# A two-layer encoder trunk: x and memory channels-first from the host, token sums by squares and a ones product, parameters packed as columns

## The chip, the core and the metric

The kernel runs on one core of a Trainium2 chip. The metric is the time of one execution on the device in microseconds, the median of the runs shown; lower is better.

## What is computed

A trunk of two layers over 256 tokens of 2048 channels (fp32), with 256 memory tokens of 2048 channels. Each layer normalises x, forms one wide projection, feeds four branches (RWKV-7 in both directions, differential attention, latent attention, attention into memory), gates them, projects each, merges them with sigmoid gates, projects again and adds the result to x. The reference, cut:

```python
def _rms_norm(t, g):
    return t * lax.rsqrt(jnp.mean(t * t, axis=-1, keepdims=True) + NORM_EPS) * g

for l in range(DEPTH):                       # DEPTH = 2
    h = _rms_norm(x, norm_g[l])
    p = h @ w_in[l]                          # 2048 -> 14784 columns, split into the branches' inputs and gates
    y_a = _rwkv7_bidir(rw_u, ...)
    y_b = ...                                # differential attention
    y_c = _mla(...)
    mem_n = _rms_norm(mem, mem_norm_g[l])    # the same memory tokens in both layers, another gain
    y_d = _mem_attention(m_q, mem_n, mem_w_kv[l], mem_qk_g[l])
    z = sum(sigmoid(merges[b]) * ((y_b_ * silu(gates[b])) @ w_branch[l, b]) for b in range(4))
    x = x + z @ w_out[l]
```

## The kernel before

**The stream of products.** `main` walks a list of jobs (`jobs`): the memory keys (memk, 16 blocks of 128 channels, 512 columns), the memory values (memv), then the products of the normalised x (U, which feeds RWKV, first), and so on through both layers. For two blocks at a time raw weights come by one 512 KB DMA on SyncE's queue (`raww`, 3 buffers, line 543). ScalarE rounds each block to `whi` (128x512) and VectorE takes the rest into `wlo`; five of each are in flight (`LOOK`). The activations are split in the same way (S0 to S3 and S4 to S7 for the memory, T1h and T1l for x), and three matmuls of hi and lo stand for one fp32 product. So a block costs six matmuls of 512 columns, or twelve of 256 in the jobs where weights are the stationary side (`product`, line 156 for every matmul; transposes are on line 161).

**What runs beside it.** Seven generators (norms, prep, xs, tables, attention, latent, rw) are stepped by a meter of the time issued so far; `yield` hands over, and a tile scheduler then orders each engine's queue by a simulated timeline. Each engine runs its own queue strictly in order. All VectorE and ScalarE work carries line 95, the meter's, so it is told apart by tile names.

**Memory.** `mem_prep` loads the memory token-major in four DMAs of 512 KB on ScalarE's queue (three into U, one into ygh), transposes 128x128 pieces on TensorE into a PSUM bank pa, and splits each into S with the gain `gains` as scale (64 transposes in two layers, of the same memory). The memory norm's scale `mrs` is not applied to S; squares of the token-major rows are summed by ScalarE (scratch T1l), and `mrs` multiplies the finished products raw and V.

**x in layer 0.** `x_prep` waits until block 3 of the memory is split, loads x token-major into Z on ScalarE's queue (line 417), sums squares on ScalarE (scratch T1h), multiplies the rows by their scale, transposes 32 pieces on TensorE and splits each from PSUM into T1h and T1l, 256 columns at a time. Layer 1 takes the same path from the x that layer 0 left on the chip. The transposes stand between the matmuls of memv and of the first U job.

**Parameters.** `params` gathers 14 small arrays as rows by GpSimd DMAs, transposes them once, and copies them to `cols`; gains are turned in the same way. The identity and other constants (`cst`) come in two DMAs at the start.

## Time and profile before

| | before |
|---|---|
| runs | 2080.51, 2083.33, 2084.84 us; median 2083.33 us |
| profiled execution: span on the core | 2081.6 us, 34016 instructions |
| its own time outside the span | not kept apart; the span lies between the lowest and the highest run |
| TensorE busy | 2052.8 us (99%), 12158 matmuls and transposes |
| VectorE, ScalarE, GpSimd busy | 68%, 54%, 6% |
| chain that ended last | TensorE 86%, issue 6%, DMA 4%, VectorE 2%, ScalarE 1% |
| DMA | 364.20 MB, mean 175 GB/s |

Busy time is the time in which an engine executes; the chain that ended last follows the work back from the last instruction, at each step to what released it. An engine that is 99% busy leaves 28.8 us of the span in which it waits; these lie in a few places, and each is read where it stands.

### The profile page before, as it was taken

The numbers are of one execution on the slowest core, as the hardware profiler recorded it, in microseconds if no ns is written. First come the engines' busy times: TensorE is split into PE (matmuls) and PEld (weight loads), VectorE is DVE, ScalarE is ACT, GpSimd is POOL, SyncE is SP. The second block draws the span as 40 slices with busy tenths as digits, with TensorE's granted clock in tenths as the row PEclk, the third lists the DMA queues.
The fourth block names the chain that finished last, engine by engine and source line by source line (L and its number), as shares of the span: only waits on it lengthen the run. The fifth ranks groups of instructions, "written<-read, shape, count | busy, mean of one in ns | idle before, by whom it ended". The sixth has DMA issues, their size and how long they took to land.

```text
span 2081.6 us, 34016 instructions
## 1 busy us (share of the span) xinstructions
PE 2052.8 (99%) x12158; PEld 1699.6 (82%) x12158; DVE 1419.1 (68%) x3073; ACT 1127.8 (54%) x2333; POOL 133.6 (6%) x168
## 2 busy tenths in 40 slices
PE   8999999999999999999999999999999999999999
PEld 6998897777877877778889988877778778777887
DVE  6787888886677577465665657666656866665654
ACT  6756575555555454445565566665555545444543
POOL 3000010110000010000000000010011001000000
PEclk9999999999999999999999999999999999999999
DMA  7655655556466566556766556555565655664565
GB/s 251 184 173 157 184 168 162 156 171 178 139 183 170 154 184 194 153 170 219 223 191 179 175 160 174 156 157 167 154 177 148 190 146 156 191 185 142 174 218 185
DMA packets 220313, 364.20 MB, mean 175 GB/s; under 512 B 40854, under 2 KB 59344, under 8 KB 219824
## 3 DMA queue, kind: packets, MB, share of 16 engines
q1 hardware_dynamic: 216528, 355.25, 58.5%
q10 hardware_dynamic: 2560, 6.30, 0.8%
q8 instruction: 95, 1.56, 0.3%
q0 software_dynamic: 1056, 0.49, 0.2%
q14 instruction: 74, 0.61, 0.1%
HBM read 354.64 MB, written 11.53 MB: 176 GB/s over the span
## 4 chain that ended last, share of the span: by engine, by line
PE 86%; issue 6%; DMA 4%; DVE 2%; ACT 1%; SPq 0%; POOL 0%; POOLq 0%; DVEq 0%; ACTq 0%
PE mm L156 75%; PE pr L156 5%; PE pa L156 3%; PE pa L161 2%; DMA BK<-sp 1%; DMA sp<-sc 1%; DVE wlo L95 1%; DMA raww<-in_mem_w_kv 1%; DMA sc<-S 0%; PE pr L161 0%; ACT whi L95 0%; DMA raww<-in_w_in 0%; DVE Z L95 0%; DVE sg L95 0%; DMA U<-in_mem 0%
## 5 line engine op out<-in xcount | busy, mean ns | idle before, releaser
L95 DVE TENSOR_TENSOR wlo<-raww,whi 128x512 fp32r<-128x512 f32 (+2 forms) x1300 | 863.7, 673 | 483.6 <-ACT whi L95 475.2
L95 ACT ACTIVATE whi<-raww 128x512 fp32r<-128x512 f32 (+2 forms) x1300 | 788.2, 617 | 730.1 <-PE mm L156 478.0
L156 PE MATMUL mm<-whi,T1l 128*128 128x512 f32 (+2 forms) x1472 | 574.8, 394 | 0.0
L156 PE MATMUL mm<-wlo,T1h 128*128 128x512 f32 (+2 forms) x1440 | 570.2, 396 | 0.5 <-DVE wlo L95 0.4
L156 PE MATMUL mm<-whi,T1h 128*128 128x512 f32 (+2 forms) x1472 | 533.6, 391 | 2.7 <-ACT whi L95 2.7
L156 PEld LDWEIGHTS mm<-whi,T1h 128*128 128x128 f32 x1472 | 278.0, 190 | 65.2 <-ACT whi L95 5.7
L156 PEld LDWEIGHTS mm<-wlo,T1h 128*128 128x128 f32 x1440 | 271.1, 188 | 62.6 <-DVE wlo L95 5.8
L156 PEld LDWEIGHTS mm<-whi,T1l 128*128 128x128 f32 x1472 | 276.5, 188 | 53.7 <-issue 2.0
L156 PE MATMUL mm<-T1l,whi 128*128 128x256 f32 x960 | 271.9, 284 | 0.0
L156 PE MATMUL mm<-T1h,wlo 128*128 128x256 f32 x960 | 270.0, 283 | 1.0 <-DVE wlo L95 0.9
L156 PE MATMUL mm<-T1h,whi 128*128 128x256 f32 x960 | 270.1, 283 | 0.0
L156 PEld LDWEIGHTS mm<-T1h,wlo 128*128 128x128 f32 x960 | 180.5, 189 | 2.3 <-DVE wlo L95 1.1
L156 PEld LDWEIGHTS mm<-T1h,whi 128*128 128x128 f32 x960 | 180.3, 188 | 1.5 <-issue 0.3
L156 PEld LDWEIGHTS mm<-T1l,whi 128*128 128x128 f32 x960 | 180.3, 188 | 1.3 <-issue 0.3
L156 PE MATMUL mm<-whi,ygh 128*128 128x512 f32 (+1 forms) x296 | 114.2, 404 | 6.1 <-ACT ygh L95 4.0
L156 PE MATMUL mm<-wlo,ygh 128*128 128x512 f32 (+1 forms) x296 | 118.5, 401 | 0.1
L156 PE MATMUL mm<-whi,ygl 128*128 128x512 f32 (+1 forms) x296 | 116.9, 397 | 0.0
L179 POOL TENSOR_TENSOR small<-small,cst 128x4 f32<-128x4 f32 (+3 forms) x46 | 52.1, 1134 | 563.5 <-DVE small L95 543.8
L156 PE MATMUL mm<-whi,S 128*128 128x512 f32 x256 | 85.0, 408 | 1.2 <-ACT S L95 0.9
L156 PEld LDWEIGHTS mm<-whi,ygh 128*128 128x128 f32 x296 | 56.6, 192 | 20.7 <-ACT ygh L95 4.6
L156 PEld LDWEIGHTS mm<-wlo,ygh 128*128 128x128 f32 x296 | 56.8, 192 | 12.4 <-DVE wlo L95 0.5
L156 PEld LDWEIGHTS mm<-whi,ygl 128*128 128x128 f32 x296 | 56.8, 192 | 12.1
(281 smaller groups left out, 2182.5 us busy)
## 6 DMA issues: line engine op xcount, KB each, us to landing
raww<-in_w_in SPq DMA_DIRECT2D x432, 512.0 KB, 3.7
raww<-in_w_branch SPq DMA_DIRECT2D x64, 512.0 KB, 3.8
raww<-in_w_out SPq DMA_DIRECT2D x64, 512.0 KB, 3.9
raww<-in_mem_w_kv SPq DMA_DIRECT2D x32, 512.0 KB, 3.8
raww<-in_w_in SPq DMA_DIRECT2D x16, 384.0 KB, 3.2
raww<-in_w_in SPq DMA_DIRECT2D x16, 320.0 KB, 3.1
raww<-in_w_in SPq DMA_DIRECT2D x16, 256.0 KB, 3.2
Z<-in_x ACTq DMA_DIRECT2D x2, 1024.0 KB, 7.8
```

Source lines behind the costliest of these rows:

```text
L95: return g(out, *args, **kw)
L156: self.nc.tensor.matmul(out, lhsT=lhsT, rhs=rhs, start=start, stop=stop)
L161: self.nc.tensor.transpose(out, in_, self.ident[:k, :k])
L179: self.nc.gpsimd.tensor_tensor(ss, ss, self.cst[:, C_MH:C_MH + n], op=ALU.pow)
```

## The change

The host hands in xT and memT, [128, 16, 256] each: channel on the partition, block of channels, token. It also hands in all of a layer's parameters as one array of columns (pcols) and both gains as columns (gcols).

- `params`: one DMA of `cols` instead of 14, a transpose and a copy. `mem_prep`: one DMA of `gains` instead of two, two transposes and two copies per layer. `setup`: `cst` comes in one DMA, issued behind the first memory loads; `ones` is now 128x2; an Exp on it stands at the start.
- `mem_prep`: X0 to X3 hold the memory channels-first and are split into S straight from SBUF; no transposes, in both layers.
- `channel_sums` (new): per quarter of the channels a square on ScalarE (128x1024), a sum over four blocks on VectorE that reads with a stride of 256 elements, a sum of the four quarters, and a product with `ones` on TensorE that sums over the partitions. It runs for x (scratch T1h, behind the load of xT) and, when that has ended (`xsum`), for the memory (scratch T1l).
- `x_first` (new, layer 0 only): four DMAs of xT into Z; sums; the scale is spread over the tokens by a copy and two transposes and copied to `r4` (named r in rows); 16 VectorE operations multiply each block by gain and scale; then eight splits of 512 columns, T1h on ScalarE, T1l on VectorE. `("hT", 0)` opens the U job when all of this has been issued.

Layer 1's `x_prep`, the jobs and their order in `jobs` are unchanged. The diff, cut to its core:

```diff
     def setup(self):
-        with self.tc.high_priority(2 * HP):
-            nc.sync.dma_start(self.cst[:, :128], a["consts"][:, :128])
-        nc.sync.dma_start(self.cst[:, 128:], a["consts"][:, 128:])
...
-        self.ones = self.cp.tile([128, 1], F32, name="ones")
+        self.ones = self.cp.tile([128, 2], F32, name="ones")
         nc.gpsimd.memset(self.ones, 1.0)
+        with self.tc.high_priority(2 * HP):
+            nc.scalar.activation(self.small(2), self.ones, AF.Exp)
...
     def params(self, l):
-        rows = self.t("kkn", [128, 256])[:P_N, :128]
-        def put(off, ap):
-            q.dma_start(rows[off:off + ap.shape[0]], ap)
-        put(P_SH, a["rw_shift"][l].rearrange("j (i p) -> (j i) p", p=128))
...
-        yield PD if l == 0 else 25.0
-        ps = self.pa()[:, :P_N]
-        self.tr(ps, rows)
         cols = self.t("cols", [128, P_N + 29])
-        nc.vector.tensor_copy(cols[:, :P_N], ps)
+        q.dma_start(cols[:, :P_N], a["pcols"][l])
+        yield PD if l == 0 else 25.0
...
     def mem_prep(self, l):
-        X3 = self.t("U", [128, 3, 2, 512])
-        X = [X3[:, j] for j in range(3)] + [self.t("ygh", [128, 2, 512])]
+        X3 = self.t("U", [128, 3, 4, 256])
+        X = [X3[:, j] for j in range(3)] + [self.t("ygh", [128, 4, 256])]
...
-            nc.sync.dma_start(rows[0], a["mem_norm_g"][l].rearrange("(k p) -> k p", p=128))
+            nc.sync.dma_start(g, a["gcols"][l])
...
-        mem = a["mem"][0].rearrange("(t p) n -> p t n", p=128)
-        q.dma_start(X[0], mem[:, :, 0:512])
+        mem = a["memT"]
+        for h in range(2):
+            q.dma_start(X[0][:, 2 * h:2 * h + 2], mem[:, 2 * h:2 * h + 2])
...
         for j in range(4):
-            for k2 in range(2):
-                i = 2 * j + k2
-                if i in (0, 2, 4):
-                    q.dma_start(X[i // 2 + 1], mem[:, :, i * 256 + 512:i * 256 + 1024])
-                ps = self.pa().rearrange("p (k t) -> p k t", k=2)
-                for k in range(2):
-                    kk = j * 4 + k2 * 2 + k
-                    for tt in range(2):
-                        self.tr(ps[:, k, tt * 128:tt * 128 + 128],
-                                X[j][:, tt, (k2 * 2 + k) * 128:(k2 * 2 + k) * 128 + 128])
-                    with self.tc.high_priority(2 * HP if kk < 4 else 0):
-                        self.split(T[j][:, k2 * 2 + k], T[4 + j][:, k2 * 2 + k], ps[:, k], scale=g[:, kk:kk + 1])
+            if j < 3:
+                q.dma_start(X[j + 1], mem[:, 4 * j + 4:4 * j + 8])
+            if j == 0 and l == 0:
+                nc.sync.dma_start(self.cst, a["consts"])
+            for k in range(4):
+                kk = j * 4 + k
+                with self.tc.high_priority(2 * HP if kk < 4 else 0):
+                    self.split(T[j][:, k], T[4 + j][:, k], X[j][:, k], scale=g[:, kk:kk + 1])
+                self.ev.add(("mT", l, kk))
...
-        yield from self.until("xsumsq")
-        ss = self.t("mss", [128, 2, 2])
-        jk = self.t("T1l", [128, 4096])
...
+        yield from self.until("xsum")
+        ss = self.t("mss", [128, 2])
+        yield from self.channel_sums(X, self.t("T1l", [128, 4096]), ss)
+        self.v["mrs"] = ss
...
+    def channel_sums(self, X, jk, rs):
+        nc = self.nc
+        sq = jk[:, 0:2048].rearrange("p (a n) -> p a n", a=2)
+        part = jk[:, 2048:3072].rearrange("p (j t) -> p j t", j=4)
+        acc = jk[:, 3072:3328]
+        for j in range(4):
+            with self.tc.issue_after(self.last[0]):
+                nc.scalar.activation(sq[:, j % 2], X[j].rearrange("p k t -> p (k t)"), AF.Square)
+            yield
+            with self.tc.issue_after(self.last[1]):
+                nc.vector.tensor_reduce(part[:, j], sq[:, j % 2].rearrange("p (k t) -> p t k", k=4), axis=AX.X,
+                                        op=ALU.add)
+            yield
+        nc.vector.tensor_reduce(acc, part.rearrange("p j t -> p t j"), axis=AX.X, op=ALU.add)
+        yield
+        ps = self.pa()
         for tt in range(2):
+            self.mm(ps[:, 2 * tt:2 * tt + 2], acc[:, tt * 128:tt * 128 + 128], self.ones)
+        nc.vector.tensor_scalar(rs, ps[:, 0:4:2], 1.0 / D, EPS, op0=ALU.mult, op1=ALU.add)
+        nc.gpsimd.tensor_tensor(rs, rs, self.cst[:, C_MH:C_MH + 2], op=ALU.pow)
+        yield
+
+    def x_first(self):
+        nc, a = self.nc, self.a
+        yield from self.until(("mload", 0))
+        X = self.t("Z", [128, 16, 256])
+        yield from self.until(("mT", 0, XK))
+        for j in range(4):
             with self.tc.issue_after(self.last[0]):
+                nc.scalar.dma_start(X[:, 4 * j:4 * j + 4], a["xT"][:, 4 * j:4 * j + 4])
+        yield XE
+        rs = self.small(2)
+        yield from self.channel_sums([X[:, 4 * j:4 * j + 4] for j in range(4)], self.t("T1h", [128, 4096]), rs)
+        self.ev.add("xsum")
+        ex = self.t("sq", [128, 2, 128])
+        nc.vector.tensor_copy(ex, rs[:, :, None].to_broadcast([128, 2, 128]))
+        ps = self.pa()[:, :256]
+        for tt in range(2):
+            self.tr(ps[:, tt * 128:tt * 128 + 128], ex[:, tt])
+        rb = self.t("r4", [128, 256], bufs=1)
+        self.copy(rb, ps)
+        yield
+        hi = self.t("T1h", [128, 16, 256], F32R)
+        lo = self.t("T1l", [128, 16, 256], F32R)
+        g = self.v["gains", 0][:, 16:32]
+        for j in range(8):
+            s = slice(2 * j, 2 * j + 2)
+            for k in (2 * j, 2 * j + 1):
+                with self.tc.issue_after(self.last[1]):
+                    nc.vector.scalar_tensor_tensor(X[:, k], X[:, k], g[:, k:k + 1], rb, op0=ALU.mult, op1=ALU.mult)
+            yield
+            self.split(hi[:, s], lo[:, s], X[:, s])
+            yield
+        self.v["hT", 0] = (hi, lo)
+        self.ev.add(("hT", 0))
```

**The opening on ScalarE.** Before, its queue has these rows where the third pair of weights is rounded and x is asked for (U, ygh and raww as above; S takes the memory's rounded part from pa, or from U and ygh after the change):

```order
L95 ACTIVATE whi_25_127<-raww_24_125 128x512
L95 ACTIVATE whi_27_131<-raww_24_125 128x512
L95 ACTIVATE whi_30_137<-raww_29_135 128x512
L95 ACTIVATE whi_35_160<-raww_29_135 128x512
L417 DMA Z_16_110<-in_x 128x2048 x2
L95 ACTIVATE S1_2_82<-pa_40_183,gains_11_91 128x256
L95 ACTIVATE S1_2_82<-pa_43_202,gains_11_91 128x256
L95 ACTIVATE whi_38_172<-raww_37_170 128x512
L95 ACTIVATE whi_41_192<-raww_37_170 128x512
L95 ACTIVATE S1_2_82<-pa_40_183,gains_11_91 128x256
```

With the change it has:

```order
L95 ACTIVATE S1_3_82<-U_10_89,gains_12_91 128x256 x4
L95 ACTIVATE whi_26_127<-raww_25_125 128x512
L95 ACTIVATE whi_30_147<-raww_25_125 128x512
L396 DMA Z_13_101<-in_xT 128x1024 x4
L95 ACTIVATE S2_4_83<-U_10_89,gains_12_91 128x256 x4
L95 ACTIVATE cols_52_260<-cols_52_260 128x2
L95 ACTIVATE S3_5_84<-ygh_11_90,gains_12_91 128x256 x4
L95 ACTIVATE whi_33_159<-raww_32_157 128x512
```

The load of x's channels has moved behind all four memory loads, and eight splits of the memory with an Exp stand between it and the fourth pair of weights.

**The seam from memv to U on TensorE.** Before, where the last memory blocks (mm_452 and mm_464, the two token halves of memv) meet the first U products (mm_750, mm_767):

```order
L156 MATMUL mm_452<-whi_633,S_4_84 128x512
L156 MATMUL mm_464<-wlo_624,S_4_84 128x512
L156 MATMUL mm_464<-whi_623,S_8_88 128x512
L156 MATMUL mm_464<-whi_633,S_4_84 128x512
L156 MATMUL mm_750<-T1h_397,whi_654 128x256
L156 MATMUL mm_750<-T1l_398,whi_654 128x256
L156 MATMUL mm_767<-T1h_397,whi_654 128x256
L156 MATMUL mm_767<-T1l_398,whi_654 128x256
L156 MATMUL mm_452<-wlo_634,S_4_84 128x512
L156 MATMUL mm_452<-whi_633,S_8_88 128x512
L156 MATMUL mm_464<-wlo_634,S_4_84 128x512
L156 MATMUL mm_464<-whi_633,S_8_88 128x512
```

With the change the same place (mm_362 and mm_373 are memv, mm_675 and mm_701 the first U products, pa_497 the turned scale of x, pa_590 the sum over partitions of the memory's squares):

```order
L156 MATMUL mm_373<-whi_502,S_5_84 128x512
L156 MATMUL mm_373<-wlo_503,S_5_84 128x512
L161 MATMUL pa_497<-cst,sq_495 128x128 x2
L156 MATMUL mm_373<-whi_502,S_9_88 128x512
L156 MATMUL mm_675<-T1h_527,whi_517 128x256
L156 MATMUL mm_701<-T1h_527,whi_517 128x256
L156 MATMUL pa_590<-ones,T1l_513 128x2 x2
L156 MATMUL mm_675<-T1l_528,whi_517 128x256
L156 MATMUL mm_675<-T1h_527,wlo_518 128x256
```

Four products of x stood ahead of the last four of memv; now the first two stand behind the last one of memv. The scale's two transposes stand ahead of that one, and the memory's two ones products behind the first two products of x.

**The same seam on VectorE.** Before, one block of x (T1l from pa) follows another between splits of the weights:

```order
L95 TENSOR_TENSOR wlo_665<-raww_652,whi_664 128x512
L95 SCALAR_TENSOR_TENSOR T1l_398<-pa_473,gains_91,T1h_397 128x256
L95 TENSOR_SCALAR rel_780<-jk_786 128x256
L95 TENSOR_TENSOR wlo_696<-raww_693,whi_695 128x512
L95 SCALAR_TENSOR_TENSOR T1l_398<-pa_511,gains_91,T1h_397 128x256
L95 TENSOR_SCALAR small_894<-small_894 128x4
L95 TENSOR_TENSOR wlo_703<-raww_693,whi_702 128x512
```

With the change (sq_495 is the spread scale of x that pa_497 turns, r is its copy on ScalarE, Z holds xT, T1l_513 is the scratch of the memory's sums, T1l_528 the low part of x):

```order
L95 TENSOR_TENSOR wlo_545<-raww_542,whi_544 128x512
L95 TENSOR_TENSOR wlo_552<-raww_542,whi_551 128x512
L95 TENSOR_REDUCE T1l_513<-T1l_513 128x256 x2
L95 SCALAR_TENSOR_TENSOR Z_101<-Z_101,gains_91,r_107_500 128x256 x12
L95 TENSOR_TENSOR wlo_672<-raww_669,whi_671 128x512
L95 SCALAR_TENSOR_TENSOR Z_101<-Z_101,gains_91,r_107_500 128x256 x2
L95 TENSOR_REDUCE T1l_513<-T1l_513 128x256
L95 SCALAR_TENSOR_TENSOR Z_101<-Z_101,gains_91,r_107_500 128x256 x2
L95 TENSOR_REDUCE T1l_513<-T1l_513 128x256
L95 TENSOR_TENSOR T1l_528<-Z_101,T1h_527 128x512 x4
L95 TENSOR_SCALAR mss_512<-pa_590 128x2
L95 TENSOR_TENSOR T1l_528<-Z_101,T1h_527 128x512 x4
```

The scaling of x, the last four sums of the memory's squares and all splits of x stand together, behind the split of the weights that are fed ahead.

**The end of layer 0's RWKV branch on TensorE** (pr rows are RWKV's, mm_9748 and mm_9759 the main stream's merge job before). Before, the products of a step (pr_9490) have main products ahead of them and behind them, before the solve with TT (pr_9521) that comes next:

```order
L156 MATMUL mm_9759<-wlo_9853,T1h_397 128x512
L156 MATMUL mm_9759<-whi_9852,T1l_398 128x512
L156 MATMUL pr_9490<-ST_76,S_1749_8278 64x128 x2
L156 MATMUL pr_9490<-X_8159,S_1751_8280 64x64
L156 MATMUL pr_9490<-X_8159,S_1752_8281 64x64
L156 MATMUL pr_9490<-X_8159,S_1751_8280 64x64
L156 MATMUL pr_9490<-X_8159,S_1752_8281 64x64
L156 MATMUL mm_9748<-whi_9864,T1h_397 128x512
L156 MATMUL mm_9748<-wlo_9865,T1h_397 128x512
L156 MATMUL mm_9748<-whi_9864,T1l_398 128x512
L156 MATMUL mm_9748<-whi_9874,T1h_397 128x512
```

With the change the last two steps (pr_9361 to pr_9536) follow each other:

```order
L156 MATMUL pr_9361<-X_8069,S_1732_8189 64x64 x4
L156 MATMUL pr_9203<-S_1734_8191,X_8069 64x64 x2
L156 MATMUL pr_9203<-S_1731_8188,ST_75 64x64 x2
L156 MATMUL pr_9400<-ST_76,S_1731_8188 64x128 x2
L156 MATMUL pr_9400<-X_8069,S_1733_8190 64x64
L156 MATMUL pr_9400<-X_8069,S_1734_8191 64x64
L156 MATMUL pr_9400<-X_8069,S_1733_8190 64x64
L156 MATMUL pr_9400<-X_8069,S_1734_8191 64x64
L156 MATMUL pr_9431<-Rs_9407,TT 64x64 x4
L156 MATMUL pr_9203<-S_1733_8190,X_8069 64x64 x2
L156 MATMUL pr_9203<-S_1731_8188,ST_76 64x64 x2
L156 MATMUL pr_9460<-X_8069,S_1732_8189 64x64 x4
```

In all, 22 main products stood ahead of pr_9490 and 12 between it and pr_9521; with the change none stands at either place of that step (pr_9400, pr_9431).

## Rows read from the trace of the kernel before

**Rows 1.** The page: busy time, share of the span and instructions of each engine, and the chain that ended last by engine and by line.

```profile
PE 2052.8 (99%) x12158; PEld 1699.6 (82%) x12158; DVE 1419.1 (68%) x3073; ACT 1127.8 (54%) x2333; POOL 133.6 (6%) x168
...
PE 86%; issue 6%; DMA 4%; DVE 2%; ACT 1%; SPq 0%; POOL 0%; POOLq 0%; DVEq 0%; ACTq 0%
```

**Rows 2.** Busy time of each engine by stretch (columns: stretch, its length, then busy us with the number of instructions begun in it for PE, PEld, DVE, ACT and POOL, the granted TensorE clock as a part of full speed, the DMA engines' busy share, GB/s).

```profile
14.00:16.00 2.00, 2.00 (x12) 1.69 (x11) 1.03 (x2) 1.15 (x2) 0.00 (x0) 1.00 0.71 127
...
880.00:884.00 4.00, 3.02 (x29) 2.65 (x30) 0.45 (x2) 1.09 (x4) 0.00 (x0) 0.50 0.02 4
...
888.00:892.00 4.00, 3.30 (x7) 2.19 (x8) 1.54 (x3) 0.93 (x2) 0.00 (x0) 0.50 0.45 118
892.00:896.00 4.00, 4.00 (x15) 3.18 (x15) 2.35 (x5) 1.20 (x2) 0.00 (x0) 0.81 0.76 280
...
900.00:1120.00 220.00, 220.00 (x1082) 182.21 (x1081) 134.86 (x229) 125.84 (x245) 8.13 (x15) 1.00 0.66 203
```

**Rows 3.** TensorE's timeline at the opening (start, length of the whole group, then the operation, its count, and in brackets the idle time before it with what ended it).

```profile
9.22 1.22 PE L156 MATMUL mm<-whi,S 128*128 128x512 f32 x2 [0.31 <-ACT whi L95]
...
18.30 0.72 PE L156 MATMUL mm<-whi,S 128*128 128x512 f32 x2
...
19.84 0.50 PE L156 MATMUL mm<-whi,S 128*128 128x512 f32 x1 [0.61 <-ACT S L95]
```

**Rows 4.** ScalarE's timeline at the opening, ACTq being its queue's DMA issues.

```profile
7.17 0.84 ACT L95 ACTIVATE S<-pa,gains 128x256 fp32r<-128x256 f32 x2
...
14.30 1.15 ACT L95 ACTIVATE whi<-raww 128x512 fp32r<-128x512 f32 x2 [1.74 <-DMA raww<-in_mem_w_kv]
15.23 0.84 ACTq L417 DMA_DIRECT2D Z<-in_x  x2
```

**Rows 5.** The chain that ended last, within the first 130 us (start, length, piece).

```profile
5.02 9.26 DMA raww<-in_mem_w_kv
...
21.04 0.22 PE pa L161 x2
...
24.28 1.40 PE mm L156 x6
```

**Rows 6.** TensorE's timeline at the seam between the last memory product and the first product of x.

```profile
61.40 0.28 PE L156 MATMUL mm<-T1h,whi 128*128 128x256 f32 x1
...
62.57 0.40 PE L156 MATMUL mm<-whi,S 128*128 128x512 f32 x1
62.80 0.28 PE L156 MATMUL mm<-T1h,wlo 128*128 128x256 f32 x1
```

**Rows 7.** VectorE's groups by line with shapes kept apart (count | busy us in all, mean ns of one | idle us before them, releaser), and two rows of its timeline, where several of a kind follow each other.

```profile
L95 DVE TENSOR_TENSOR wlo<-raww,whi 128x512 fp32r<-128x512 f32 x1192 | 811.6, 689 | 450.4 <-ACT whi L95 442.9 <-PE mm L156 2.7 <-ACT Rs L95 1.0
...
L95 DVE TENSOR_REDUCE small<-pa 128x2 f32<-128x512 f32 x16 | 10.9, 683 | 3.6 <-PE pa L156 3.5
...
L95 DVE SCALAR_TENSOR_TENSOR S<-kkn,G 128x256 f32<-128x256 f32 x16 | 9.6, 598 | 0.0
...
70.09 3.10 DVE L95 TENSOR_TENSOR wlo<-raww,whi 128x512 fp32r<-128x512 f32 x5
73.11 0.87 DVE L95 SCALAR_TENSOR_TENSOR T1l<-pa,gains,T1h 128x256 fp32r<-128x256 f32 x2
```

**Rows 8.** ScalarE's groups, in the same columns.

```profile
L95 ACT ACTIVATE whi<-raww 128x512 fp32r<-128x512 f32 x1192 | 738.2, 630 | 688.5 <-PE mm L156 438.7 <-DVE wlo L95 90.2 <-DMA raww<-in_w_in 80.9
...
L95 ACT ACTIVATE S<-pa,gains 128x256 fp32r<-128x256 f32 x32 | 14.6, 465 | 5.2 <-PE pa L161 4.5 <-PE mm L156 0.7
...
L95 ACT ACTIVATE V<-mm 128x512 f32<-128x512 f32 x8 | 4.6, 591 | 1.7 <-PE mm L156 1.5
...
L95 ACT ACTIVATE T1l<-U 128x1536 f32<-128x1536 f32 x2 | 3.0, 1488 | 0.0
...
L95 ACT ACTIVATE raw<-raw,mrs 128x512 f32<-128x512 f32 x4 | 2.8, 713 | 1.9 <-POOL mrs L179 1.9
...
L95 ACT ACTIVATE T1l<-ygh 128x512 f32<-128x512 f32 x2 | 1.2, 618 | 0.0
```

**Rows 9.** GpSimd's timeline where the memory tokens' scale is raised to its power.

```profile
51.85 0.90 POOL L179 TENSOR_TENSOR mrs<-mrs,cst 128x2 f32<-128x2 f32 x1
```

**Rows 10.** TensorE's groups of transposes, in the columns of rows 7.

```profile
L161 PE MATMUL pa<-cst,Z 128*128 128x128 f32 x180 | 30.5, 273 | 0.0
...
L161 PE MATMUL pa<-cst,U 128*128 128x128 f32 x48 | 10.0, 298 | 1.6 <-DVE S L95 1.6
...
L161 PE MATMUL pa<-cst,ygh 128*128 128x128 f32 x16 | 2.9, 272 | 0.0
```

**Rows 11.** The chain near the end of layer 0's RWKV branch (start, length, piece), and TensorE's timeline right behind it.

```profile
877.69 0.28 DVE ST L95
...
879.09 0.68 PE pr L156 x12
...
879.79 0.28 ACT Rs L95
...
880.12 0.72 PE pr L156 x8
...
888.94 0.63 PE L156 MATMUL mm<-wlo,ygh 128*128 128x512 f32 x1
889.37 0.63 PE L156 MATMUL mm<-whi,ygh 128*128 128x512 f32 x1
```

More of the change, by code (lines that the diff above doesn't have):

```diff
@@ L353, in mem_prep @@
         T = [self.t(f"S{i}", [128, 4, 256], F32R) for i in range(8)]
-        X3 = self.t("U", [128, 3, 2, 512])
-        X = [X3[:, j] for j in range(3)] + [self.t("ygh", [128, 2, 512])]
+        X3 = self.t("U", [128, 3, 4, 256])
+        X = [X3[:, j] for j in range(3)] + [self.t("ygh", [128, 4, 256])]
         q = nc.scalar if l == 0 else nc.sync
         g = self.t("gains", [128, 32])
-        rows = [self.t("Rs", [16, 128], bufs=2) for i in range(2)]
         with self.tc.high_priority(2 * HP):
-            nc.sync.dma_start(rows[0], a["mem_norm_g"][l].rearrange("(k p) -> k p", p=128))
+            nc.sync.dma_start(g, a["gcols"][l])
@@ L361, in mem_prep @@
         self.v["mT", l] = T
[L362 to L363 removed]
+        self.v["gains", l] = g
+        mem = a["memT"]
+        for h in range(2):
+            q.dma_start(X[0][:, 2 * h:2 * h + 2], mem[:, 2 * h:2 * h + 2])
         self.ev.add(("mload", l))
[L365 to L370 removed]
@@ L389, in mem_prep @@
-        gains(1)
+        for j in range(4):
+            if j < 3:
[7 more added lines that the diff above has]
+                self.ev.add(("mT", l, kk))
+                if k % 2:
+                    yield 0.0
@@ L398, in mem_prep @@
             yield
-            with self.tc.issue_after(self.last[0]):
-                self.sumsq(X[3][:, tt], ss[:, tt, 1:2], jk[:, 2048:2560])
+            self.split(hi[:, s], lo[:, s], X[:, s])
             yield
-        rs = self.t("mrs", [128, 2])
-        nc.vector.tensor_reduce(rs, ss, axis=AX.X, op=ALU.add)
-        self.rsqrt(rs, 2, 1.0 / D, EPS)
-        self.v["mrs"] = rs
-        self.ev.add("mrs")
+        self.v["hT", 0] = (hi, lo)
+        self.ev.add(("hT", 0))
     def x_prep(self, l):
@@ L410, in x_prep @@
         if l == 0:
-            yield from self.until(("mload", 0))
-            X = self.t("Z", [128, 2, 2048])
-            SS = self.t("xss", [128, 2, 4])
-            yield from self.until(("mT", 0, XK))
-            for tt in range(2):
-                with self.tc.issue_after(self.last[0]):
-                    nc.scalar.dma_start(X[:, tt], a["x"][0, tt * 128:tt * 128 + 128, :])
-            yield XE
-            jk = self.t("T1h", [128, 4096])
-            nc.vector.memset(SS, 0.0)
-            for tt in range(2):
-                with self.tc.issue_after(self.last[0]):
-                    self.sumsq(X[:, tt], SS[:, tt, 0:1], jk[:, tt * 2048:tt * 2048 + 2048])
-                yield
-            self.ev.add("xsumsq")
-        else:
-            yield from self.until(("x", l))
-            X, SS = self.v["x", l], self.v["ss", l]
+            yield from self.x_first()
+            return
+        yield from self.until(("x", l))
+        X, SS = self.v["x", l], self.v["ss", l]
         g = self.v["gains", l][:, 16:32]
@@ L1138, in rw_unit @@
             cum = self.t("r2", [128, 4, 64], bufs=2)
-            ones = self.ones.to_broadcast([128, 64])
+            ones = self.ones[:, 0:1].to_broadcast([128, 64])
             for c in range(4):
@@ L1455, with _columns, c, _channels_first @@
     Builder(ctx, tc, aps).build()
+def _columns(a):
+    def c(v):
+        return v.reshape(-1, 128)
+    both, gains = [], []
+    for l in range(L):
+        dq = a["diff_qk_g"][l]
+        both.append(np.concatenate([
+            c(a["rw_shift"][l]), c(a["rw_w0"][l]), c(a["rw_a0"][l]), c(a["rw_k_k"][l]), c(a["rw_k_a"][l]),
+            c(a["rw_r_k"][l]), c(a["rw_gn_g"][l]), c(a["rw_gn_b"][l]), np.concatenate([dq, dq], axis=1),
+            c(a["diff_sub_g"][l]), c(a["mla_q_lat_g"][l]), c(a["mla_kv_lat_g"][l]), a["mla_nope_g"][l],
+            a["mem_qk_g"][l]]).T)
+        gains.append(np.concatenate([c(a["mem_norm_g"][l]), c(a["norm_g"][l])]).T)
+    return np.ascontiguousarray(np.stack(both)), np.ascontiguousarray(np.stack(gains))
+def _channels_first(t):
+    return np.ascontiguousarray(t.T.reshape(KT, 128, S).transpose(1, 0, 2))
 _INS = ["x", "mem", "positions", "norm_g", "w_in", "rw_shift", "rw_w0", "rw_w_up", "rw_a0", "rw_a_up",
@@ L1471 @@
     given["consts"] = _constants()
+    given["pcols"], given["gcols"] = _columns(given)
+    given["xT"], given["memT"] = _channels_first(given["x"][0]), _channels_first(given["mem"][0])
+    for n in _PACKED:
+        del given[n]
     for n, v in given.items():
```

25 lines of the change are left out of this document (3 added, 22 removed).

## The prediction

> **What bounds the kernel now.** I read the page first: TensorE is busy for 2052.8 of 2081.6 us and holds 86% of the chain that ended last [rows 1]. So each TensorE operation taken away can be worth its time, and each wait put into TensorE's queue costs its time, since no slack is left to swallow it: in layer 1's memory stage it is busy for 220.00 of 220.00 us [rows 2]. Where TensorE waits now I read from the timeline of the first 20 us and from the end of layer 0's RWKV branch. At the opening the first product starts at 9.22 and the seventh block waits until 19.84 for ScalarE's split of the memory [rows 3]; behind it the chain is nearly TensorE alone, with a block of six matmuls at 1.40 us and two transposes at 0.22 [rows 5]. At the seam from the memory products to those of x there is no wait: four x products run from 61.40, the last memv product from 62.57, x again from 62.80 [rows 6]. Around 880 to 892 the engine waits on RWKV and the granted clock falls to 0.50 [rows 2].
>
> The sum is made against the profiled span, 2081.6 us, 1.7 below the median of the runs (2083.33); the difference is added to that median.
>
> **TensorE work that goes.** Memory transposes: 64 [rows 10], 32 per layer; of x's 180, 32 go. At 0.11 each [rows 5] that is 10.4 us, and ones products and the scale's transposes give back about 0.9. Layer 1's part is plain: 32 transposes and two of gains, 3.8 us, in a stretch where TensorE is always busy. **Term 1: -3.8.** GpSimd's DMAs, the earlier constants and the parameters' copy lie beside weights and hide; without that cover each would cost a DMA's latency, and only the opening lacks cover. Layer 0's part is in the terms below, by when U begins.
>
> **The opening.** ScalarE's queue now loads all four memory quarters, and its four issues for xT stand ahead of the last eight memory splits. The first of these issues waits for the last memory quarter. Up to it the queues carry three weight pairs, four memory quarters (512 KB each) and the constants. The same loads were in flight before, and the third weight pair, the last of them, landed at 5.02 + 9.26 = 14.28 [rows 5], after which the rate fell to 127 GB/s [rows 2]. So this quarter lands at about 14 (estimate; 12.5 if it gets its share sooner). Then ScalarE needs 1.7 for four issues (two took 0.84 [rows 4]), eight splits at 0.37 (0.84 for two is 0.47 + 0.37) = 3.0, and 0.6 for the weights' split [rows 8] with two hand-overs: block 6 starts at 19.4, against 18.30 [rows 3]. From there 26 blocks (156 matmuls of 512 columns at 1.40/6 = 0.233) take 36.4, with 0.4 for ones and transposes: memv ends at **t0 = 56.2**. Before it ended at 62.8 [rows 6]; 0.47 of U had run by then, but 20 of x's 32 transposes (2.2) still stood behind in the queue, so for U it stood as at 64.5. Up to here the change is 8.3 us ahead.
>
> **The seam.** This is where it is lost. TensorE's queue holds two ones products for the memory's sums behind the second U product, and the 30 others of these two blocks behind them. They need the last sum on VectorE, and VectorE has put the scaling of x in between. TensorE's transposes of the scale are the last but one thing before t0, so r cannot come sooner. From t0: ScalarE takes out memv's first half at -0.5 (0.59) and rounds the fifth block by 0.0; squares of two quarters until 0.95 and 1.9 (512 elements took 618 ns, 1536 took 1488 [rows 8]: 1024 about 1.05, 0.95 following another), r at 2.3. VectorE: wlo 0.65; a quarter's sum of 1024 elements is 1.2 if it goes as 683 ns for 512 [rows 7], less what overlaps; two until 3.35; 12 scalings at 0.40 (0.87 for two is 0.47 + 0.40 [rows 7]) until 8.1; wlo 8.7; two scalings 9.5; the ygh quarter's sum 10.7; two scalings 11.5; the last sum 12.6. Ones products until 13.0, first T1l (0.69) 13.7. Of this 0.24 is covered by the two U products: TensorE waits about 13.4. Nothing else stands ready in its queue. **Rows for the clock:** after the RWKV wait matmuls of 512 columns followed each other at 0.43 (888.94 to 889.37 [rows 11]) and the clock was 0.50 until 892 and 0.81 to 896 [rows 2]; 10 to 12 such at 0.2 more are 2.4 here. So U stands as at 56.2 + 13.7 - 0.24 + 2.4 = 72.1, against 64.5. **Term 2: +7.6.**
>
> Bounds of the seam: from r at 0.5 and no wait for squares, 16 scalings, two wlo's, two sums and the rest make 10.6; if the strided sums take 2.2 each (twice), four of them add 4.4. I take 13.4, since the nearest strided row, 598 ns against 0.47 for the same operation on contiguous data [rows 7], shows a quarter more, not double.
>
> [...]
>
> **Behind the seam.** VectorE makes the memory's scale only after four T1l, GpSimd needs 0.90 [rows 9], then ScalarE has four products to scale (0.71 each [rows 8]) and two squares ahead of the next weights. Five blocks of U (7.0 us) are ready and cover most: **term 3: +1** (0 to 3).
>
> **RWKV's end in layer 0.** The queue now has the last but one step without main products in its gaps. In the last step of before these gaps are 877.69 to 879.09 (four state copies) and 879.77 to 880.12 [rows 11]: 1.4 + 0.35, at a clock that may already be falling. **Term 4: +2** (0 where RWKV comes early, 3.5 where both remaining steps pay). In layer 1 the rows are the same as before: nothing.
>
> Sum: -3.8 + 7.6 + 1 + 2 = **+6.8**, so 2083.3 + 6.8 = **2090 us**.
>
> **Rivals.**
> 1. *Faster: the seam costs little.* TensorE is the bound and work is removed; if VectorE's sums and scalings ran ahead of t0, TensorE would lose only what is behind the last transposes. Price: without seam wait and clock, -8.3 - 3.8 + 3 = -9.1, 2074. For it: 99% busy. Against it: the order of VectorE's queue, and r behind pa_497. It decides when the wait at t0 and its clock stay under about 4.8 us together (15.8 - 4.8 = 11 less gives -4.2). Chance 0.12.
> 2. *No change.* The last quarter lands at 12.5, block 6 at 17.9 (-1.5); the seam at its lower bound (-2.8); no backlog and no RWKV cost (-3): about 2083. For it: each bound taken alone is possible. Against: all at once are needed. Chance 0.20.
> 3. *Strided sums twice as long:* +4.4 at the seam, 2094 to 2095; if also the memory splits in layer 1, which stand ahead of other work while their load lands, held up weights, some 2 more. Chance 0.18.
> 4. *The forecast*, a seam that costs more than the transposes gave: 0.50.
>
> [...]
>
> **How the numbers follow.** About 0.2% (4.2 us) is what a measurement of this kernel tells from no change. Faster than 2079.2: rival 1, 0.12. Within: rival 2 and a little of the forecast's lower edge, 0.21. Slower than 2087.5: 0.67. The range reaches from 2079, where rival 1 begins, to 2098, rival 3 with its addition; it leaves out 0.12 below and some 0.06 above. The forecast's own range is 2087 to 2094.
>
> **What would show it.** In the changed profile: block 6 at 18 to 20; last memv product at 55 to 58; at pa_590 a TensorE wait of 12 to 15 us with VectorE's T1l sum as its releaser, in which VectorE is busy throughout; granted clock 0.5 behind it; T1l sums at 1.1 to 1.3 us (2.2 or more for rival 3); no pa transposes of memory from 990 to 1040; a chain with VectorE's Z in it. The prediction is wrong if TensorE's wait at the seam is under 8 us, if block 6 comes after 22, or if RWKV's end in layer 0 differs by more than 5 us.

## The result, and the profile after

The changed kernel takes 2101.21 us (median; 2098.17 to 2102.17) against 2083.57 for the kernel before on the same chip: ratio 1.0082, 95% interval 1.0066 to 1.0097, so some +17 us where +6.8 was forecast. Its profiled span is 2096.4 us against 2081.6: +14.8; the profiled execution is the fastest of its four, so the trace shows some 3 us less of the loss than the medians. Slower was right, the size was not; 2101 lies above the range (2079 to 2098). One disturbed execution (e2's first, 5490.49 us) is left out of all medians and ratios.

The page of the changed kernel, engines and chain, to be held against [rows 1]:

```profile
PE 2038.3 (97%) x12066; PEld 1697.2 (81%) x12066; DVE 1437.0 (69%) x3075; ACT 1126.2 (54%) x2323; POOL 124.2 (6%) x142
...
PE 82%; issue 6%; DMA 5%; DVE 4%; ACT 2%; SPq 0%; POOL 0%; ACTq 0%; DVEq 0%; POOLq 0%
```

TensorE is busy for 14.5 us less, yet the span is longer: it waits. Gaps over 0.15 us add up to 23.6 us before and to 53.0 after. To see where, the main stream's products (9144) are counted in both traces, and the end of the n-th before is taken from its end after:

| stretch | forecast | measured |
|---|---|---|
| to product 400 (opening, seam, backlog: terms 2 and 3) | +8.6 | +14.7 |
| 400 to 3600 | 0 | +5.9 |
| 3600 to 4000 (RWKV's end, term 4) | +2 | +6.9 |
| 4000 to 4600 (layer 1's memory, term 1) | -3.8 | -7.0 |
| 4600 to 6200 | 0 | +3.5 |
| 6200 to the end | 0 | -9.1 |
| sum | +6.8 | +14.9 |

How far such a count differs by itself shows where two kernels have the same work: the two executions of e1 (below) differ by up to 2.4 us in one stretch, and e5, whose edit lies in layer 1, differs by 2.2 from the changed kernel up to product 400.

**The opening**, first ScalarE's timeline (ACTq: its DMA issues):

```profile
14.71 0.33 ACTq L396 DMA_DIRECT2D Z<-in_xT  x1
...
15.66 1.76 ACTq L396 DMA_DIRECT2D Z<-in_xT  x3
17.46 1.71 ACT L95 ACTIVATE S<-U,gains 128x256 fp32r<-128x256 f32 x4 [1.88 <-issue]
...
19.17 1.69 ACT L95 ACTIVATE S<-ygh,gains 128x256 fp32r<-128x256 f32 x4
```

then TensorE's, which answers to [rows 3] (the first product starts at 7.24 instead of 9.22):

```profile
18.05 0.40 PE L156 MATMUL mm<-whi,S 128*128 128x512 f32 x1
21.45 0.73 PE L156 MATMUL mm<-whi,S 128*128 128x512 f32 x2 [2.99 <-ACT whi L95]
...
24.23 0.63 PE L156 MATMUL mm<-wlo,S 128*128 128x512 f32 x1
24.66 0.63 PE L156 MATMUL mm<-whi,S 128*128 128x512 f32 x1
```

The first load of x is issued at 14.71, the last three from 15.66 to 17.42, and only then come the eight splits: block 6 starts at 21.45, not at 19.4. In the built program the four issues wait in turn for the last memory quarter, for the two loads of the positions and for the table of relative positions, earlier loads that the same four semaphores count. Behind the wait of 2.99 us some products follow each other at 0.43, half the pace (granted clock 0.50 from 23.5 to 26).

**The seam** on TensorE, against [rows 6]:

```profile
60.41 0.48 PE L156 MATMUL mm<-whi,S 128*128 128x512 f32 x1
67.13 0.79 PE L156 MATMUL mm<-T1h,whi 128*128 128x256 f32 x2 [6.24 <-ACT T1h L95]
76.31 0.98 PE L156 MATMUL pa<-ones,T1l 128*128 128x2 f32 x4 [8.39 <-DVE T1l L95]
78.14 0.58 PE L156 MATMUL mm<-T1l,whi 128*128 128x256 f32 x1 [0.84 <-DVE T1l L95]
```

and on VectorE:

```profile
61.87 3.75 DVE L95 TENSOR_REDUCE T1l<-T1l 128x256 f32<-128x1024 f32 x2 [0.25 <-ACT T1l L95]
65.53 4.84 DVE L95 SCALAR_TENSOR_TENSOR Z<-Z,gains,r 128x256 f32<-128x256 f32 x12
70.28 0.69 DVE L95 TENSOR_TENSOR wlo<-raww,whi 128x512 fp32r<-128x512 f32 x1
70.88 0.88 DVE L95 SCALAR_TENSOR_TENSOR Z<-Z,gains,r 128x256 f32<-128x256 f32 x2
71.67 1.90 DVE L95 TENSOR_REDUCE T1l<-T1l 128x256 f32<-128x1024 f32 x1
73.48 0.88 DVE L95 SCALAR_TENSOR_TENSOR Z<-Z,gains,r 128x256 f32<-128x256 f32 x2
74.27 1.90 DVE L95 TENSOR_REDUCE T1l<-T1l 128x256 f32<-128x1024 f32 x1
77.39 1.90 DVE L95 TENSOR_TENSOR T1l<-Z,T1h 128x512 fp32r<-128x512 f32 x3 [1.23 <-PE pa L156]
```

Up to the last sum VectorE works through the forecast's list without a gap, piece by piece in its order; then the first T1l waits 1.23 us for the ones products. TensorE waits 6.24 + 8.39 + 0.84 = 15.5 us. The windows of 4 us (columns as in [rows 2]) show the granted clock, 0.50 ahead of the first T1l product and 0.86 in the window in which U comes into full stream:

```profile
72.00:76.00 4.00, 0.00 (x0) 0.00 (x0) 4.00 (x4) 1.06 (x2) 0.00 (x0) 0.50 0.03 4
...
80.00:84.00 4.00, 4.00 (x31) 4.00 (x31) 2.37 (x4) 2.85 (x7) 1.08 (x1) 0.86 0.00 0
```

**RWKV's end.** The first main product behind it (the 3919th) on TensorE's timelines before and after:

```profile
888.35 0.79 PE L156 MATMUL mm<-whi,ygh 128*128 128x512 f32 x1 [2.01 <-ACT ygh L95]
```

```profile
910.70 0.80 PE L156 MATMUL mm<-whi,ygh 128*128 128x512 f32 x1 [2.01 <-ACT ygh L95]
```

It starts 22.35 us later; 20.6 of that was lost by product 3600, so RWKV's end itself costs 1.8. The other 5.1 of the stretch come behind it. The chain, ScalarE's, VectorE's and TensorE's timelines there, one row or two of each:

```profile
911.13 5.67 DMA U<-in_memT
```

```profile
916.83 0.91 ACT L95 ACTIVATE S<-U,gains 128x256 fp32r<-128x256 f32 x2 [6.09 <-DMA U<-in_memT]
917.65 0.61 ACT L95 ACTIVATE whi<-raww 128x512 fp32r<-128x512 f32 x1
```

```profile
917.37 0.64 DVE L95 SCALAR_TENSOR_TENSOR S<-U,gains,S 128x256 fp32r<-128x256 f32 x1 [3.45 <-ACT S L95]
917.94 0.68 DVE L95 SCALAR_TENSOR_TENSOR sg<-sg,mm 128x512 f32<-128x512 f32 x1
```

```profile
918.67 0.50 PE L156 MATMUL mm<-whi,ygh 128*128 128x512 f32 x1 [1.62 <-DVE sg L95]
...
926.72 0.50 PE L156 MATMUL mm<-wlo,T1h 128*128 128x512 f32 x1 [2.02 <-DVE wlo L95]
```

Layer 1's first memory split stands at the head of ScalarE's and VectorE's queues until its load lands, and a weights split and the gates (sg) stand behind it.

### The profile page after: what moved, and what is told of

The parts are those of the page before. It is cut to its first block, busy times and chain, and to the rows that moved or that the text cites. A ratio compares the mean times of both kernels' runs of the same rounds, so it can differ in the third digit from the quotient of the medians.

```text
span 2096.4 us, 33755 instructions
## 1 busy us (share of the span) xinstructions
PE 2038.3 (97%) x12066; PEld 1697.2 (81%) x12066; DVE 1437.0 (69%) x3075; ACT 1126.2 (54%) x2323; POOL 124.2 (6%) x142
## 4 chain that ended last, share of the span: by engine, by line
PE 82%; issue 6%; DMA 5%; DVE 4%; ACT 2%; SPq 0%; POOL 0%; ACTq 0%; DVEq 0%; POOLq 0%
PE mm L156 72%; PE pr L156 5%; PE pa L156 3%; PE pa L161 2%; DMA BK<-sp 1%; DVE wlo L95 1%; DMA raww<-in_w_in 1%; DMA sp<-sc 1%; DMA sc<-S 1%; ACT whi L95 1%; DVE S L95 1%; DMA q<-in_positions 0%; DVE Z L95 0%; PE pr L161 0%; DVE T1l L95 0%
## 5 line engine op out<-in xcount | busy, mean ns | idle before, releaser
L156 PE MATMUL mm<-whi,T1l 128*128 128x512 f32 (+2 forms) x1472 | 567.5, 389 | 0.0
L156 PE MATMUL mm<-T1h,wlo 128*128 128x256 f32 x960 | 274.4, 287 | 0.1
L156 PEld LDWEIGHTS mm<-whi,S 128*128 128x128 f32 x256 | 49.9, 197 | 22.0 <-ACT whi L95 11.1
L156 PEld LDWEIGHTS mm<-wlo,ygh 128*128 128x128 f32 x296 | 56.2, 190 | 12.5 <-DVE wlo L95 1.0
```

Of the source, the lines that this page charges most:

```text
L156: self.nc.tensor.matmul(out, lhsT=lhsT, rhs=rhs, start=start, stop=stop)
```

## Experiments

The theory after this reading: strided sums, a late block 6 and memory splits that wait for a load make the loss. The rival: x's own chain from load to first T1l makes it, whatever else is moved. And since the last third of the kernel, whose work is the same, ran 9 us faster, a second theory: the tiles' places in on-chip memory (SBUF) set the pace of the products. Ratios are to the kernel before on the same chip; where two ratios are subtracted, each difference carries the width of both intervals, some 4 us.

**What the strided sums cost** (e3). Edit, in `channel_sums`:

```diff
-tensor_reduce(part[:, j], sq[:, j % 2].rearrange("p (k t) -> p t k", k=4), ...)
+tensor_reduce(part[:, j], sq[:, j % 2].rearrange("p (t k) -> p t k", k=4), ...)
```

(The sum of the four quarters is read in a row in the same way.)

> The changed kernel, but each sum over 1024 elements adds four neighbours in place of four elements 1 KB apart, so the token sums are not those of the reference; nothing else is changed. Theory (the stride makes the sum 1.9 us long): the sums take 1.2 us, the four at the seam give 2.8 us: about 2098 us. Rival (1024 elements take 1.9 us however they lie): 1.9 us and 2101 us.

Measured: ratio 1.0065 (1.0044 to 1.0086), by whole times not told from the changed kernel's 1.0082; the trace decides. VectorE's groups by shape, of the changed kernel and of this one:

```profile
L95 DVE TENSOR_REDUCE T1h<-T1h 128x256 f32<-128x1024 f32 x5 | 10.1, 2020 | 0.0
L95 DVE TENSOR_REDUCE T1l<-T1l 128x256 f32<-128x1024 f32 x5 | 9.5, 1927 | 0.3 <-ACT T1l L95 0.3
```

```profile
L95 DVE TENSOR_REDUCE T1l<-T1l 128x256 f32<-128x1024 f32 x5 | 6.0, 1215 | 0.3 <-ACT T1l L95 0.3
```

In a row a sum takes 1.21 us, which the forecast had used; with the stride 1.93 to 2.02. TensorE's waits at the seam fall from 15.5 to 12.7 us (4.82 + 7.04 + 0.84): 2.8 of the loss. The forecast's 13.4 is near the seam of this kernel, not of the changed one.

**The memory's sums behind x** (e2, run a second time for its profile).

```diff
-        yield from self.until("xsum")
+        yield from self.until(("hT", 0))
-        yield from self.channel_sums(X, self.t("T1l", [128, 4096]), ss)
+        yield from self.channel_sums(X, self.t("Z", [128, 4096]), ss)
```

(`r4` is padded to 264 so that T1l keeps its place.)

> The changed kernel, but the sums of the memory's squares wait until x is split (scratch in Z in place of T1l), so they no longer stand between x's scaling and the first U products; T1l's place is kept as in the changed kernel. Theory (the seam's loss is the queue order: the memory's ones products and sums ahead of x): TensorE's waits at the seam fall from 15.5 us to 2 to 5, the time by 9 to 13: 2088 to 2092 us. Rival (the sums and the scaling of the memory's products have to be done anyway, and delay U's weights behind the seam): under 4 us gained, 2097 or more.

> The changed kernel with the memory's sums behind the products of x, for its profile at the seam. Theory (the memory's sums stood ahead of x on VectorE and of U on TensorE): no ones product of the memory between the first two U products, TensorE's waits from the last memory value product to a full stream of U 6 to 9 us instead of 15.5. Rival (x's own chain takes all of it): 12 us or more.

Measured: ratio 1.0014 (1.0001 to 1.0026), 14 us less than the changed kernel (10 to 18 by the intervals). The profiled execution, 2086.36 us, is a single one, at 1.0027 of before. TensorE's timeline at the seam:

```profile
65.34 0.80 PE L156 MATMUL mm<-T1h,whi 128*128 128x256 f32 x2 [4.22 <-ACT T1h L95]
71.03 0.58 PE L156 MATMUL mm<-T1l,whi 128*128 128x256 f32 x1 [4.89 <-DVE T1l L95]
```

The waits are 9.1 us instead of 15.5: outside the 2 to 5 of the first expectation and at the edge of the second's 6 to 9. x's own scaling, 14 operations in 5.77 us ahead of the first T1l, makes most of them. Part of the 4.22 us is not x's: ahead of r ScalarE has the load of a function table (1.28 us from 60.63) and operations of the position tables, which now come before the seam. To product 400 the gain is 7.5, 2.6 more up to product 3600 and 2.8 at RWKV's end, which here loses nothing (-1.0); the spans differ by 11.9.

**Block 6 earlier** (e7). x's load waits for all 16 memory splits (two padded tiles keep T1h and T1l at their place to the weights):

```diff
-        yield from self.until(("mT", 0, XK))
+        yield from self.until(("mT", 0, KT - 1))
```

> The changed kernel, but the four loads of x's channels are issued behind all splits of the memory and not ahead of the last eight; T1h and T1l lie to the weights as in the changed kernel. Theory (ScalarE's issues and their waits hold the memory's splits up): the wait for block 6 (2.99 us) shrinks to under 1.5 and the low clock behind it goes, 2 to 4 us: 2097 to 2099 us. Rival (block 6 waits for weights or the memory's load): the wait stays within 0.5 us of 3, 2101 us or more, since x arrives later.

Measured: 1.0076 (1.0059 to 1.0093), not told from 1.0082. TensorE's timeline:

```profile
19.59 0.72 PE L156 MATMUL mm<-whi,S 128*128 128x512 f32 x2 [1.29 <-ACT whi L95]
...
77.17 0.99 PE L156 MATMUL pa<-ones,T1l 128*128 128x2 f32 x4 [4.79 <-DVE T1l L95]
79.00 0.58 PE L156 MATMUL mm<-T1l,whi 128*128 128x256 f32 x1 [0.84 <-DVE T1l L95]
```

Block 6 comes at 19.59 and the memory products end 2.4 us sooner, yet U is in full stream at 79.00 instead of 78.14: x came later, and ahead of the T1l wait TensorE now waits 3.04 + 3.81 + 4.95 us for x's sum, its spread and its first split. A miss for the theory that the opening's 4.7 us were a loss by themselves: what the opening gains, x's late chain takes at the seam.

**Layer 1's memory splits behind weights splits** (e5):

```diff
+        if l:
+            yield 10.0
...
+                if l:
+                    with self.tc.issue_after(self.last[0]):
+                        self.split(T[j][:, k], T[4 + j][:, k], X[j][:, k], scale=g[:, kk:kk + 1])
+                else:
                     with self.tc.high_priority(2 * HP if kk < 4 else 0):
```

> The changed kernel, but in layer 1 each split of the memory is issued behind a split of the weights, some 10 us later, in place of directly behind the end of layer 0's RWKV branch; all tiles lie where they lie in the changed kernel. Theory (the splits wait for the memory's load at the head of ScalarE's and VectorE's queues, and the weights behind them are late): the two TensorE waits behind RWKV's end (1.6 and 2.0 us in the profile of the changed kernel) and the low clock after the second go, 4 to 5 us: 2096 to 2097 us, 1.006 of before. Rival (all of the loss in that stretch is RWKV's own step without main products): unchanged, 1.008.

Measured: 1.0041 (1.0026 to 1.0056), 8.5 us less than the changed kernel (4 to 13 by the intervals, so the expected 4 to 5 is not ruled out). From product 3600 to 4000 the loss is 0.9 instead of 6.9; ScalarE's timeline has a weights split where it waited 6.09 us for the load:

```profile
913.57 0.63 ACT L95 ACTIVATE whi<-raww 128x512 fp32r<-128x512 f32 x1 [2.92 <-PE mm L156]
```

The first main product behind RWKV's end starts at 910.61, as late as in the changed kernel, so that part (1.8) stays; what goes is the loss behind it. The other runs (e4, e6, e9 and e10 follow below) agree, in us against the kernel before:

| | from product 3600 to the first one behind RWKV's end | from there to product 4000 |
|---|---|---|
| memory's sums ahead of x, splits at the queues' head (changed kernel, e3, e7, e9) | +1.6 to +2.5 | +2.9 to +5.1 |
| memory's sums ahead of x, splits moved (e5) | +1.8 | -0.9 |
| memory's sums behind x, splits at the queues' head (e2, e4) | -1.0 | +5.2 to +6.0 |
| memory's sums behind x, splits moved (e6, e10) | -0.9 to -0.7 | -0.9 to -0.1 |

Between runs that differ by this edit (the changed kernel and e5, e4 and e10; e2 and e6, which differ by e7's edit as well) the second column differs by 6.0, 5.3 and 6.9. So the load at the head of two queues costs 5 to 7 us. RWKV's own end costs 1.6 to 2.5, but only where the memory's sums stand ahead of x; why it hangs on them was not tried.

**All three together** (e6: the edits of e2, e5 and e7, T1h and T1l at the weights' place within 256 bytes).

> The changed kernel with the memory's sums behind x's split (as e2), layer 1's splits spread between the weights' (as e5) and the load of x's channels behind all memory splits (as e7); T1h and T1l lie to the weights as in the changed kernel. Theory (the three places are the loss, and they add up): e2's 1.0014 of before, less 4 to 5 us for the splits and 2 to 3 for the opening: 0.997 to 0.9985 of before, and TensorE's wait at the seam is 2 to 6 us. Rival (each mended wait is taken up by another): 1.001 or more.

Measured: 1.0001 (0.9992 to 1.0010): as the kernel before, between the theory (0.997 to 0.9985) and its rival (1.001 or more). Beside e1 below (0.9973), which is the kernel before with T1l at the weights' place, it is still 6 to 7 us longer. TensorE's waits at its seam:

```profile
62.62 0.58 PE L156 MATMUL pa<-ones,T1h 128*128 128x2 f32 x4 [2.89 <-DVE T1h L95]
...
65.03 0.69 PE L161 MATMUL pa<-cst,sq 128*128 128x128 f32 x2 [1.83 <-DVE sq L95]
...
67.83 0.80 PE L156 MATMUL mm<-T1h,whi 128*128 128x256 f32 x2 [2.11 <-ACT T1h L95]
73.25 0.58 PE L156 MATMUL mm<-T1l,whi 128*128 128x256 f32 x1 [4.63 <-DVE T1l L95]
```

11.5 us in x's own chain alone, not 2 to 6: here the rival holds. The first two waits, 4.7 us, came with e7's edit: in e2, where x is loaded earlier, its ones products (53.80) and its turn (60.51) stand ahead of the seam. e2's edit with e5's alone was not tried. Sum, power, spread, turn and 16 scalings are one series, whose end TensorE awaits; token-major, before, a token's scale lay on the token's own partition and multiplied the rows ahead of the turn, long before the seam.

**The places of tiles** (e1: the kernel before with T1l moved by 128 bytes in each partition; e9: the changed kernel with T1l moved by 128, in the same way).

```diff
-        ss = self.t("mss", [128, 2, 2])
+        ss = self.t("mss", [128, 36])[:, 0:4].rearrange("p (a b) -> p a b", a=2)
```

> The kernel before, with nothing changed but that a scratch tile ahead of T1l is 128 bytes larger, so that T1l and all tiles behind it lie 128 bytes higher. The traces show matmuls of 512 columns with T1l following each other at 234 ns before and 227 ns after the change, those with wlo and T1h at 232 and 227, and tiles lie at other places in the two. Theory A (the pitch hangs on where weights and activations lie to each other, modulo 256 bytes; here T1l comes to the same place as the weights): both pitches fall to 227, 1343 x 7 + 1312 x 5 ns = 16 us less: 2067 us (2064 to 2070). Rival (the pitch follows from the order of instructions or the run): 234 and 232 stay, 2083 us.

> The changed kernel, with only a tile ahead of T1l 152 bytes larger, so that T1l and all tiles behind it lie 128 bytes higher: the opposite of e1. Theory A (places modulo 256 bytes): matmuls of 512 columns with T1l go from 227 to 232 or 234 ns, those with wlo and T1h to 232, those of 256 columns from 120 back to 118 or 119: between 6 us (what e1 gained by whole times) and 11 us (its count) slower than the changed kernel: 1.011 to 1.0135 of before. Rival: pitches stay at 227 and 120, 1.008.

In the built programs `whi`, `wlo` and T1h start 64 bytes past a multiple of 256 before and T1l 192; with the change all four start at 160. e1 puts T1l to 64, e9 to 32. The attention's tiles behind T1l move with it. Measured: e1 0.9973 (0.9959 to 0.9986), which is 6 us and not the 16 of theory A; e9 1.0115 (1.0099 to 1.0130), 0.33% above the changed kernel and within its expectation. The same 64 products of T1h and T1l, from the first to the product that follows them, on TensorE's timelines of the kernel before, e1 (its second run), the changed kernel and e9:

```profile
1966.19 0.48 PE L156 MATMUL mm<-wlo,T1h 128*128 128x512 f32 x1
...
1981.07 0.62 PE L156 MATMUL mm<-whi,ygh 128*128 128x512 f32 x2
```

```profile
1957.90 0.48 PE L156 MATMUL mm<-wlo,T1h 128*128 128x512 f32 x1
...
1972.52 0.62 PE L156 MATMUL mm<-whi,ygh 128*128 128x512 f32 x2
```

```profile
1983.41 0.47 PE L156 MATMUL mm<-wlo,T1h 128*128 128x512 f32 x1
...
1998.04 0.64 PE L156 MATMUL mm<-whi,ygh 128*128 128x512 f32 x2
```

```profile
1985.07 0.48 PE L156 MATMUL mm<-wlo,T1h 128*128 128x512 f32 x1
...
1999.96 0.62 PE L156 MATMUL mm<-whi,ygh 128*128 128x512 f32 x2
```

14.88 and 14.62 us, 14.63 and 14.89: the place decides, in both directions, not the change. Products of 256 columns go the other way; from 1130 to 1160, the windows of the products on mm alone (columns as in [rows 2], without POOL), in the kernel before and in e1's second run:

```profile
1130.00:1160.00 30.00, 30.00 (x257) 30.00 (x256) 3.57 (x8) 1.74 (x4) 1.00 0.64 184
```

```profile
1130.00:1160.00 30.00, 30.00 (x252) 30.00 (x251) 3.57 (x8) 1.76 (x4) 1.00 0.56 173
```

By counts of each pair of products and its median distance, the change's places are worth some -13 us (about -18 at 512 columns in T1h, T1l and the attention's tiles, +4.6 at 256). The runs give back less: e9's span is 3.7 us above that of the changed kernel, its ratio some 7; its other waits are 4.2 us shorter, so its span less waits is 8 above. e1's spans are 12.0 and 9.1 below the kernel before, its ratios 6 to 7 us, where the count says 9.3. So by e9 some 7, by the count 13 us of the change's loss were hidden; which of them stays open.

**What the memory transposes are worth** (e4: x in layer 0 as before, the memory's sums behind it, memory and parameters as in the change, T1l at the weights' place by a padded tile; e10: e4 with e5's edit; e1 once more on e10's chip).

> The changed kernel with x of layer 0 as it was before (token-major load, squares on ScalarE, 32 transposes); memory channels-first and packed parameters stay, the memory's sums come after x is split (scratch in Z). T1l is placed to lie like T1h and the weights. Theory (the memory's part of the change gains its transposes, x's part loses at the seam): no wait of over 3 us at the seam, memory transposes gone, so 8 to 12 us under the kernel of e1 for 64 transposes at 0.11 to 0.16, less 4 for layer 1's memory load ahead of the splits: 2058 to 2068 us. Rival (the memory's load and sums cost as much as its transposes): 2070 to 2085 us.

> Layer 0's x as before (token-major, transposed), memory channels-first in both layers with the memory's sums after x, parameters in columns, T1h and T1l at the weights' place within 256 bytes, and in layer 1 each split of the memory issued behind a split of weights. Theory (the 64 memory transposes are a gain of their own once no queue waits for the layer 1 load): the end of layer 0's RWKV branch costs at most 2 us instead of e4's 4.3, and the whole is 0.9955 to 0.997 of the kernel before, below e4's 0.9982 and below the kernel before with T1l moved alone. Rival (what transposes give back at TensorE is always lost at another wait): 0.9975 to 0.9985, no better than the tile's move alone.

> The kernel before with T1l moved by 128 bytes per partition, on the same chip as e10. Both theories: 0.996 to 0.9985 as the first time (0.9973). If e10 is not below this run, the transposes gave nothing that lasts.

Measured: e4 0.9982 (0.9969 to 0.9994), 2077.69 us, no better than e1's 0.9973: the rival's range, and a miss for the theory's 2058 to 2068. e10 0.9957 (0.9945 to 0.9969), 2072.65 us, beside e1 at 0.9968 (0.9957 to 0.9980), 2074.38 us. e10 beats both kernels; from e1 it is not told apart. Between these two traces the layer 1 memory stage gains 4.7 us and the stretch with RWKV's end loses 0.3, as the theory has it, but e10 loses 1.9 to product 400 and 3.0 from there to 3600. Its chain and TensorE's timeline at the opening:

```profile
14.97 10.38 DMA raww<-in_mem_w_kv
```

```profile
26.14 1.22 PE L156 MATMUL mm<-whi,S 128*128 128x512 f32 x2 [7.58 <-ACT whi L95]
```

The products run 2 to 3 us ahead of e1's (the first at 7.22 instead of 9.39) and then wait 7.58 us for weights. Whether the transposes give back anything that lasts is thus not shown by whole times.

## Why the forecast was short

**Term 2, the opening's part: failed by 4.7.** The step that failed is "The first of these issues waits for the last memory quarter", with the other three straight behind it. The first went at 14.71 (about 14 was forecast), but the second waited until 15.63 for the load of the positions, which its semaphore counts as well; the chain shows that release and no run moved that load. The last issue ended at 17.42 instead of 15.7, and the eight splits took 3.4 instead of 3.0. That makes 2.05 us. Another 2.6 went behind the wait of 2.99 us, some 1.5 of it at half clock, which the forecast had charged at the seam but not here. The memory products end at 60.9, not at 56.2. e7 shows that mending it by a later load of x brings nothing, since x is late then.

**Term 2, the seam's part: mechanism right, +3.5 mis-sized.** The sum term, "a quarter's sum of 1024 elements is 1.2", measured 1.93, and 1.21 in a row (e3): 2.8 of it; the ones products took 0.98 at half clock (0.50 from 76 to 78) instead of 0.4. The factor of 1.6 lies between forecast and rival 3. No run shows the sums of 2.2 us that rival 3 and the upper bound take; with the stride the changed kernel showed means of 1.93 us (T1l) and 2.02 (T1h). The row that had been taken for strided (598 ns, [rows 7]) is no measure for it: G's elements lie next to each other in runs of 64. The clock's 2.4 us were 1.2, since products of 256 columns lose 0.09 each (0.21 us apart from 78.5 to 80.9, then 0.12), not 0.2.

**Term 3** was nothing instead of 1. 4.7 + 3.5 - 1.2 - 1 = 6.0 explains the first line of the table (6.1).

**Term 4: RWKV's own end was right, +1.8 for +2; the wait of layer 1's splits was left out, 5.1.** It was in the text, but under rival 3, at "some 2", with "if". The queues' order showed layer 1's memory splits ahead of the last weights splits; the step that failed was to let that wait decide only in a rival. A load that lands 5.67 us after its issue makes two gaps of 1.62 and 2.02 on TensorE and a slower clock behind the second (0.62 from 928 to 932); with the splits moved (e5) the loss there is gone.

**Term 1: the mechanism was right**, -3.8 forecast. The stretch gained 7.0; with T1l moved back (e9) it gains 4.7, as e10 does beside e1, so some 4.7 are the transposes and 2.3 the tiles' places.

**What had no term.** From product 400 to 3600 TensorE has 5.9 us of waits more, at five places (229.17, 451.74, 455.12, 630.91 and 809.77; 2.77 + 1.39 + 0.65 + 0.84 + 1.13, less 0.93 that stood before), each for a split of weights; what delays these was not tried. e3, e5 and e7, whose edits lie elsewhere, lose 3.1 to 3.6 there, and the waits at 630.91 and 809.77 stand in none of them, so some 2.5 belong to this execution. From 4600 to 6200 the +3.5 is 2.1 us of pace (products of 256 columns at 120 ns; in e9 it is gone) and 1.4 of waits; of the -9.1 behind it 7.6 are pace and 1.5 waits. The tiles' places, which no view of the trace of before shows as such, gave some 7 to 13 us back. Without them the change costs 25 to 31 us (an estimate: 17.6 by the medians plus these), about four times the forecast.

**The rivals.** Rival 1 (TensorE is the bound and work is removed) ends 27 us off: e10 shows 4.7 us for the transposes in layer 1, where TensorE waits for nothing, and a loss in the opening. Rival 3 came nearest, with its sums (2.9 of the +4.4) and its layer 1 splits (5.1 for 2), both sized wrongly.

**The signs.** VectorE busy throughout ahead of the memory's ones products, the granted clock of 0.50 behind them and Z in the chain came as named. Block 6 (21.45 for 18 to 20), the last memory product (60.9 for 55 to 58) and the sums (1.93 for 1.1 to 1.3) did not.
